# Segment mean over sorted ids: the preparation of the bridges of more groups moved from GpSimd to VectorE

## The chip, the cores and the metric

One core of one Trainium2 chip runs the kernel. The metric is the device time of one execution in microseconds (us); the figure for a kernel is the median of its runs.

## What is computed

```python
data = np.random.randn(10_000_000).astype(np.float32)
segment_ids = np.sort(np.random.randint(0, 10000, 10_000_000))
np.add.at(sums, segment_ids, data)
np.add.at(counts, segment_ids, 1)
return sums / np.maximum(counts, 1)
```

The ids are sorted, so a segment is a run of neighbouring elements. The output is one mean for each of the 10,000 segments.

## The kernel before, in words

Each of the 128 partitions holds 78,125 neighbouring elements. They are cut into 90 rows of 875 elements; two rows are one data tile, and there are 45 tiles, 23 even ones and 22 odd ones. The kernel treats a row as holding at most one border between two segments; whether it does is told from samples of the ids ("probes", every 175th id). It has to know at which column of each row the border lies. Then VectorE makes one masked sum per row (`split`, line 662, 90 instructions of 875 columns), and ScalarE makes the plain sum of each tile (`total`, line 650, 45 instructions).

The column of a border is found with the ids themselves, but only with the short stretch of them in which it must lie. For an even tile's row this is `first_look`: a few small VectorE instructions (lines 431 to 475) work out from the probes the address of a window of 175 ids in every partition and write it to IDX; GpSimd then issues an indirect DMA for that row (`gather`, line 415), and ScalarE sums the ids that land (`add_ids`, line 502). `second_look` (line 513, VectorE) turns the sum into the column KK of the border. For an odd tile's row no window is looked up from probes alone: a **bridge** is laid between the even tiles on both sides. `bridge` (lines 566 to 613, VectorE) draws a line between the columns of the neighbours, which gives the address of a window of 232 ids (IDX, line 605); GpSimd gathers it, ScalarE sums it, and `bridged` (line 624, VectorE) makes the column of it.

The rows are taken in nine groups of up to three even tiles (GROUPS, line 41). Group g has an even part, `look`, `ids` and `second`, and, from group 1 on, an odd part, `prepare`, `bridge`, `xids` and `bridged`, for the odd tiles between its even tiles and those of the group before. The gathers of one full part are six indirect DMAs. In the text, "even 5" is the even part of group 5 and "odd 4" the odd part of group 4.

`prepare(i, j)` (lines 521 to 555) makes four small tiles that `bridge` needs and that hang on the probes alone: LN, SM, FB and WV, 128 partitions by 4 or 6 columns. It has two forms. If `i < EARLY`, VectorE makes them in four instructions (lines 532 to 540). Otherwise GpSimd makes them in six (lines 545 to 553). Here i is the number of the first odd tile of the group. With line 1274, `put(f"prepare{g}", prepare(o0, o1))`, and line 1268, `o0, o1 = max(i - 1, 0), j - 1`, it is 0, 2, 5, 8, 11, 14, 17 and 20 for groups 1 to 8. With EARLY = 5 (line 162), groups 1 and 2 are prepared by VectorE and groups 3 to 8 by GpSimd.

```python
            if i < EARLY:
                v = nc.vector
                v.tensor_scalar(
                ...
                return
            e = nc.gpsimd
```

The order of work on every engine is written out by hand. TIMES (lines 42 to 152) gives each step a number, and the steps are put in the order of these numbers; the whole part of a number is the split after which the step comes, so that "prepare4" at 22.02 stands right behind "second4" at 22.02, and ahead of the third step of "look5" at 22.035. An engine runs its own instructions in that order. On GpSimd, the gathers of a part and the six instructions of a `prepare` stand in one queue: prepare 3 stands between the gathers of even 4 and of odd 3, and prepare 4 between those of odd 3 and of even 5.

The gathers write into a ring of 18 slots (GT). The data tiles come into 16 buffers by SyncE's queue, in the order of ORDER (line 36), with the loads of the probes among them. After the last split the pieces are put together: TensorE folds shifted copies (lines 1058 to 1074), `hits` (lines 634 to 642) and `spread` (line 1129) come on GpSimd behind the last gathers, and `ends` (line 1227) on VectorE writes the last columns of the output.

Of the kernel before, what the change touches and what calls it, by code (L numbers as in the profile page):

```python
# [158 lines left out]
R1 = 8 * M1 - 2  # L159
R2 = NR + 4  # L160
RM = 74
EARLY = 5
LATE = [r for r in range(RM, NR, 4)]
C1, CA, C2 = 31, 67, 48

# [70 lines left out]
def kernel(  # L236
# [68 lines left out]
    def view(ap, dims):  # L305
        return bass.AP(ap.tensor, ap.offset, [list(ap.ap[0])] + dims)
# [214 lines left out]
    def prepare(i, j):  # L521

        def s1():
# [5 lines left out]
            ids = view(pr32[:, 4 * i + 2, 0:1], [[8 * K, n], [2 * K, 2]])  # L529
            if i < EARLY:  # L530
                v = nc.vector
# [822 lines left out]
```

## Time and profile before

| | us |
|---|---|
| median of 3 runs | 186.96 |
| lowest and highest run | 186.78, 187.04 |
| the profiled execution | 187.27 |
| its span, first to last instruction | 185.5 |
| outside the span | 1.8 |

Busy within the span: VectorE 138.3 us, ScalarE 122.9, GpSimd 115.5, TensorE 15.9.

In the profile's rows, PE is TensorE's matmuls, DVE is VectorE, ACT ScalarE, POOL GpSimd, and SP SyncE; L415 is line 415 of the kernel. Times are us from the start of the span. A row of a timeline begins with start and duration; what stands in brackets at its end is the time for which the engine sat idle just before, and what ended that. A wait that the profile can't put down to an instruction is called "issue". A gather's duration on POOL is the time in which its descriptors are written, not that in which its bytes arrive.

### The profile page before, as it was taken

The numbers are of one execution on the slowest core, as the hardware profiler recorded it, in microseconds if no ns is written. First come the engines' busy times: TensorE is split into PE (matmuls) and PEld (weight loads), VectorE is DVE, ScalarE is ACT, GpSimd is POOL, SyncE is SP. The second block draws the span as 40 slices with busy tenths as digits, with TensorE's granted clock in tenths as the row PEclk, the third lists the DMA queues.
The fourth block names the chain that finished last, engine by engine and source line by source line (L and its number), as shares of the span: only waits on it lengthen the run. The fifth ranks groups of instructions, "written<-read, shape, count | busy, mean of one in ns | idle before, by whom it ended". The sixth has DMA issues, their size and how long they took to land.

```text
span 185.5 us, 1564 instructions
## 1 busy us (share of the span) xinstructions
PE 15.9 (9%) x72; PEld 15.6 (8%) x72; DVE 138.3 (75%) x466; ACT 122.9 (66%) x290; POOL 115.5 (62%) x166
## 2 busy tenths in 40 slices
PE   0000000000000000010000000000000065009900
PEld 0000000000000000010000000000000065009900
DVE  6314396980349999192999999696999999699980
ACT  8503655640599995392997985567889686989700
POOL 5474757787577287777468777737838788552400
DMA  5999999999999999999999999999999999940000
GB/s 110 114 272 287 202 264 399 238 410 344 341 394 334 350 396 334 339 331 337 404 328 340 394 329 386 388 398 411 411 403 402 397 408 404 409 207 0 0 4 12
DMA packets 47685, 56.71 MB, mean 306 GB/s; under 512 B 37664, under 2 KB 38104, under 8 KB 47671
## 3 DMA queue, kind: packets, MB, share of 16 engines
q1 hardware_dynamic: 41739, 40.32, 65.8%
q0 software_dynamic: 5760, 16.26, 26.1%
q14 instruction: 13, 0.11, 0.2%
q10 hardware_dynamic: 172, 0.00, 0.1%
q8 instruction: 1, 0.02, 0.0%
HBM read 58.97 MB, written 0.04 MB: 318 GB/s over the span
## 4 chain that ended last, share of the span: by engine, by line
DMA 36%; issue 18%; POOL 15%; ACT 11%; DVE 8%; PE 5%; SPq 4%; POOLq 0%; DVEq 0%; ACTq 0%
DMA GT<-in_segment_ids_dram,IDX 32%; POOL GT L415 11%; ACT junk_a L650 6%; ACT junk_i L502 5%; PE outp L1070 5%; DMA pr<-in_segment_ids_dram 4%; DVE junk_v L662 4%; SPq L272 3%; SPq L290 1%; POOL xa L1129 1%; SPq L277 1%; DVE most L1203 1%; DVE pa L1112 0%; POOL bad L875 0%; DVE j L838 0%
## 5 line engine op out<-in xcount | busy, mean ns | idle before, releaser
L415 POOL DMA_INDIRECT GT<-in_segment_ids_dram,IDX x90 | 92.8, 1031 | 46.0 <-issue 24.2
L662 DVE SCALAR_TENSOR_TENSOR junk_v<-iota,q,data_t 128x875 bf16<-128x875 f32 x90 | 98.8, 1116 | 0.3 <-DVE SG L458 0.2
L650 ACT ACTIVATE junk_a<-data_t 128x1750 bf16<-128x1750 f32 (+1 forms) x45 | 73.7, 1639 | 1.1 <-issue 0.7
L502 ACT ACTIVATE junk_i<-GT 128x175 bf16<-128x175 int32 (+1 forms) x90 | 33.6, 374 | 49.6 <-DMA GT<-in_segment_ids_dram,IDX 46.7
L502 ACT ACTIVATION_READ_ACCUMULATOR junk_i<-GT 128x1 f32 x90 | 16.8, 187 | 0.0
L513 DVE SCALAR_TENSOR_TENSOR q<-YY,GS 128x6 f32<-128x6 f32 (+2 forms) x9 | 1.5, 169 | 16.8 <-ACT junk_i L502 14.6
L1058 PE MATMUL outp<-tab,diag 128*128 128x79 f32 x24 | 5.4, 424 | 66.3 <-DVE tab L1038 66.3
L1058 PEld LDWEIGHTS outp<-tab,diag 128*128 128x128 f32 x24 | 5.2, 331 | 66.4 <-DVE tab L1038 66.4
L1070 PE MATMUL outp<-xa,ident 128*128 128x36 f32 x40 | 8.7, 408 | 11.1 <-POOL xa L1129 11.1
L1070 PEld LDWEIGHTS outp<-xa,ident 128*128 128x128 f32 x40 | 8.6, 332 | 11.3 <-POOL xa L1129 11.3
L431 DVE TENSOR_TENSOR q<-pr 128x12 f32<-128x12 int32 (+3 forms) x9 | 1.6, 176 | 10.1 <-DMA pr<-in_segment_ids_dram 9.8
L650 ACT ACTIVATION_READ_ACCUMULATOR junk_a<-data_t 128x1 f32 x45 | 8.4, 187 | 0.0
L769 PE MATMUL small<-q,ident 128*128 128x100 f32 x2 | 0.7, 464 | 82.8 <-DVE q L761 82.8
L769 PEld LDWEIGHTS small<-q,ident 128*128 128x128 f32 x2 | 0.5, 314 | 82.8 <-POOL WV L553 82.8
L624 DVE TENSOR_TENSOR q<-ZV,GS 128x6 f32<-128x6 f32 (+1 forms) x8 | 1.3, 166 | 8.2 <-ACT junk_i L502 8.2
L662 DVE DVE_READ_ACCUMULATOR junk_v<-iota,q,data_t 128x1 f32 x90 | 7.4, 82 | 0.0
L308 ACT ACTIVATE GT<-q 128x4176 int32<-128x4176 f32 x1 | 3.9, 3894 | 0.0
L681 DVE TENSOR_TENSOR q<-T,q 128x10 f32<-128x10 f32 (+3 forms) x5 | 2.1, 412 | 1.5 <-ACT junk_a L650 1.5
L1157 POOL TENSOR_TENSOR pb<-pb,RB 128x620 f32<-128x620 f32 x1 | 1.3, 1315 | 2.2 <-DVE RB L937 2.2
L638 POOL TENSOR_TENSOR uu<-uu,GS 128x44 f32<-128x44 f32 x1 | 0.3, 279 | 3.3 <-ACT junk_i L502 3.3
L1196 POOL TENSOR_TENSOR add<-gg,XX 128x620 f32<-128x620 f32 x1 | 1.3, 1302 | 1.4 <-DVE XX L1189 1.4
L1047 DVE TENSOR_TENSOR diag<-ident,dm 128x1664 f32<-128x1664 f32 x1 | 1.9, 1891 | 0.0
(159 smaller groups left out, 84.0 us busy)
## 6 DMA issues: line engine op xcount, KB each, us to landing
data_t<-in_data_dram SPq DMA_DIRECT2D x44, 875.0 KB
GT<-in_segment_ids_dram,IDX POOLq DMA_INDIRECT x90
data_t<-in_data_dram SPq DMA_DIRECT2D x1, 562.5 KB
pr<-in_segment_ids_dram SPq DMA_DIRECT2D x22, 11.0 KB
pr<-in_segment_ids_dram SPq DMA_DIRECT2D x3, 6.0 KB
out_dram<-OUT SPq DMA_DIRECT2D x1, 36.6 KB
pr<-in_segment_ids_dram SPq DMA_DIRECT2D x1, 4.0 KB
snt<-in_segment_ids_dram ACTq DMA_DIRECT2D x1, 1.0 KB
```

The lines of the kernel that those rows point to most:

```text
L272: nc.sync.dma_start(out=pr_flat[:, a:b], in_=ids_p[:, a * S : (b - 1) * S + 1 : S])
L277: nc.sync.dma_start(out=pr_flat[:, a:b:w], in_=ids_p[:, a * S : (b - 1) * S + 1 : w * S])
L290: nc.sync.dma_start(out=d[:, 0 : b - a], in_=data_p[:, a:b])
L308: nc.scalar.activation(out=gt32[:, :, 0 : 2 * WO : 2], in_=view(q5[:, 0, 0:1], [[0, RING], [0, WO]]), func=ACT.Copy)
L415: nc.gpsimd.indirect_dma_start(out=GT[:, slots[r], 0:w], out_offset=None, in_=ids2d[:], in_offset=bass.IndirectOffsetOnAxis(ap=IDX[:, r : ...
L502: nc.scalar.activation(out=turned(junk_i)[:, 0:w], in_=gt32[:, slots[r], 0 : 2 * w : 2], func=ACT.Copy, accum_out=GS[:, r : r + 1],)
L650: nc.scalar.activation(out=junk_a[:, 0:n], in_=tiles[t][:, 0:n], func=ACT.Copy, accum_out=T[:, 2 * t : 2 * t + 1])
L662: nc.vector.scalar_tensor_tensor(out=turned(junk_v)[:, 0:n], in0=iota[:, 0:n], scalar=KK[:, r : r + 1], in1=d, op0=ALU.is_ge if r % 2 else ...
L681: nc.vector.tensor_sub(out=odd(A), in0=even(T), in1=even(A))
L1047: nc.vector.tensor_tensor(out=diag, in0=view(ident[:, 0:1], [[0, ND], [1, P]]), in1=view(dm[:, 0:1], [[1, ND], [0, P]]), op=ALU.mult,)
L1058: nc.tensor.matmul(out=outp[:, 0:NO], lhsT=diag[:, d], rhs=tab[:, d : d + NO], start=d == 0, stop=False)
L1070: nc.tensor.matmul(out=outp[:, C1:CA], lhsT=ident[:, 0:P], rhs=xa[:, :, r - R1], start=False, stop=False)
```

## The change

One constant is raised from 5 to 9:

```diff
@@ -159,7 +159,7 @@
 R1 = 8 * M1 - 2
 R2 = NR + 4
 RM = 74
-EARLY = 5
+EARLY = 9
 LATE = [r for r in range(RM, NR, 4)]
 C1, CA, C2 = 31, 67, 48
```

The constant is used in one place, the condition in `prepare` that is quoted above. It was announced as: the bridges of the last four groups, too, are prepared by VectorE in four fused steps instead of six on GpSimd; nothing else is changed.

## Rows read from the trace of the kernel before

**Rows 1.** The waits of the whole span: who, for whom, total, times, longest
```profile
ACT junk_i L502 <- DMA GT<-in_segment_ids_dram,IDX: 46.7, 30, 9.1
DVE q L513 <- ACT junk_i L502: 14.6, 4, 8.2
```

**Rows 2.** The chain that ended last: start, duration, what
```profile
79.64 7.90 DMA GT<-in_segment_ids_dram,IDX
...
119.34 7.28 DMA GT<-in_segment_ids_dram,IDX
...
155.28 7.82 DMA GT<-in_segment_ids_dram,IDX
```

**Rows 3.** Windows: us, PE, PEld, DVE, ACT, POOL busy, PEclk, DMA share, GB/s
```profile
70.00:80.00 10.00, 0.00 (x0) 0.00 (x0) 5.61 (x15) 4.83 (x17) 7.57 (x13) 1.00 1.10 324
160.00:170.00 10.00, 3.29 (x16) 3.29 (x16) 8.04 (x27) 9.38 (x18) 4.18 (x8) 1.00 0.47 191
```

**Rows 4.** The page's part on DMA queues: the gathers' queue, packets, MB, share
```profile
q0 software_dynamic: 5760, 16.26, 26.1%
```

**Rows 5.** Timeline of VectorE: instructions that waited, over the middle of the span
```profile
55.42 0.17 DVE L624 TENSOR_TENSOR q<-ZV,GS 128x4 f32<-128x4 f32 x1 [2.35 <-ACT junk_i L502]
...
78.33 0.20 DVE L624 TENSOR_TENSOR q<-ZV,GS 128x6 f32<-128x6 f32 x1 [4.36 <-ACT junk_i L502]
...
88.10 0.21 DVE L513 SCALAR_TENSOR_TENSOR q<-YY,GS 128x6 f32<-128x6 f32 x1 [3.32 <-ACT junk_i L502]
...
118.61 0.17 DVE L624 TENSOR_TENSOR q<-ZV,GS 128x6 f32<-128x6 f32 x1 [1.44 <-ACT junk_i L502]
...
127.19 0.18 DVE L513 SCALAR_TENSOR_TENSOR q<-YY,GS 128x6 f32<-128x6 f32 x1 [1.37 <-ACT junk_i L502]
...
162.30 0.17 DVE L681 TENSOR_TENSOR q<-T,q 128x10 f32<-128x10 f32 x1 [1.47 <-ACT junk_a L650]
```

**Rows 6.** Line 545, the first of GpSimd's six: durations, first and last start
```profile
L545 POOL TENSOR_SCALAR LN<-NBP x6: 195/204/206, 58.2 to 146.5; 128x6 f32<-128x6 f32 x5, 128x4 f32<-128x4 f32 x1
```

**Rows 7.** Timeline of GpSimd: around prepare 3 and prepare 4
```profile
63.23 1.12 POOL L415 DMA_INDIRECT GT<-in_segment_ids_dram,IDX  x1 [3.44 <-DVE IDX L605]
...
69.88 1.00 POOL L415 DMA_INDIRECT GT<-in_segment_ids_dram,IDX  x1 [0.30 <-issue]
70.95 0.20 POOL L545 TENSOR_SCALAR LN<-NBP 128x6 f32<-128x6 f32 x1
...
73.01 1.10 POOL L415 DMA_INDIRECT GT<-in_segment_ids_dram,IDX  x1 [0.59 <-DVE junk_v L662]
...
79.64 1.00 POOL L415 DMA_INDIRECT GT<-in_segment_ids_dram,IDX  x1 [0.30 <-issue]
```

**Rows 8.** Timeline of VectorE: prepare 2 begins, and the instruction behind it
```profile
25.84 0.16 DVE L532 TENSOR_SCALAR LN<-NBP 128x6 f32<-128x6 f32 x1
...
26.13 0.16 DVE L470 SCALAR_TENSOR_TENSOR ST<-NBP,ST 128x6 f32<-128x6 f32 x1
```

**Rows 9.** Timeline of VectorE: addresses of even 5, bridge 4's last steps
```profile
68.48 0.17 DVE L475 SCALAR_TENSOR_TENSOR IDX<-ST,wb 128x6 int32<-128x6 f32 x1
...
80.63 0.17 DVE L599 TENSOR_SCALAR CC<-CC 128x6 f32<-128x6 f32 x1
...
80.83 0.17 DVE L605 SCALAR_TENSOR_TENSOR IDX<-CC,FB 128x6 int32<-128x6 f32 x1
```

**Rows 10.** Timelines: a long VectorE instruction, and the gather beside it
```profile
38.27 1.89 DVE L1047 TENSOR_TENSOR diag<-ident,dm 128x1664 f32<-128x1664 f32 x1
...
38.50 2.54 POOL L415 DMA_INDIRECT GT<-in_segment_ids_dram,IDX  x1 [0.30 <-issue]
```

**Rows 11.** Timeline of ScalarE: last id sums of even 5 and even 7, one total
```profile
87.62 0.36 ACT L502 ACTIVATE junk_i<-GT 128x175 bf16<-128x175 int32 x1 [2.67 <-DMA GT<-in_segment_ids_dram,IDX]
...
109.78 1.66 ACT L650 ACTIVATE junk_a<-data_t 128x1750 bf16<-128x1750 f32 x1 [0.72 <-issue]
...
126.71 0.36 ACT L502 ACTIVATE junk_i<-GT 128x175 bf16<-128x175 int32 x1 [0.95 <-DMA GT<-in_segment_ids_dram,IDX]
```

## The prediction

> **What bounds the kernel now.** I read four views in this order: the waits, the chain that ended last, the windows, and then the timelines of VectorE, GpSimd and ScalarE around the places where the change works.
>
> The waits show a loop. ScalarE waits 46.7 us in 30 times for gathered ids to land, and VectorE then waits 14.6 us in 4 times for ScalarE's sum of them [rows 1]. The chain that ended last runs through the same loop: it contains the last gather of even 5, issued at 79.64 and landed 7.90 us later, that of even 7 at 119.34 (7.28 us) and that of odd 8 at 155.28 (7.82 us) [rows 2]. VectorE writes addresses, GpSimd issues six gathers, they land, ScalarE sums, VectorE works out the next addresses. The reader is to see that this latency is the bound, and that no engine's share of busy time is.
>
> The second candidate is the transfer as such. From 70 to 80 us the DMA engines are busy all the time (share 1.10) [rows 3]. But they are done early: from 160 to 170 the share is 0.47 [rows 3], so the data stream ends near 165, while the span runs to 185.5. And in the middle VectorE's idle time before its waiting instructions ends with a sum of ScalarE, not with a data tile [rows 5]. I take the loop to be the bound, and the stream to be close behind it.
>
> **What the change does.** The text announces the last four groups. The code says otherwise: the condition compares i, the first odd tile, with EARLY, and i is 0, 2, 5, 8, 11, 14, 17, 20. Raising 5 to 9 moves the groups with i = 5 and i = 8, that is groups 3 and 4, and leaves the last four (11 to 20) on GpSimd. Before, line 545 runs 6 times [rows 6]; after, it must run 4 times. Twelve small GpSimd instructions go and eight VectorE instructions come. No DMA and no other instruction moves.
>
> **Removed from GpSimd, prepare 3.** It stands ahead of the gathers of odd 3. The first of these waits at 63.23, after 3.44 us of idleness, for VectorE's address [rows 7]. Taking away work ahead of a wait of 3.44 us gains nothing: 0.
>
> **Removed from GpSimd, prepare 4.** It stands between the last gather of odd 3 and the first of even 5. The former begins at 69.88 and takes 1.00, so GpSimd is free at 70.88; prepare 4 starts at 70.95, and the next gather only at 73.01 [rows 7]. Without it the next gather starts after the usual pause of 0.30 us [rows 7], at 71.18. Its address is not what it waits for: line 475 is done at 68.65 [rows 9]. So the first gather of even 5 is issued 73.01 - 71.18 = 1.83 us sooner. The last one follows five gathers later, each 1.00 with a pause of 0.30 [rows 7]: 71.18 + 5 x 1.30 = 77.68 instead of 79.64. The first gather after other work takes 1.10 instead of 1.00 [rows 7], and that goes too. I count **1.9 us** for the issue of the last gather.
>
> **Added to VectorE.** Prepare 2 has this form already: four instructions from 25.84, and the next one starts at 26.13 [rows 8], so 0.29 us each time, 0.6 us together. Prepare 3 comes behind split 13, right ahead of the 2.35 us in which VectorE waits for odd 1 until 55.42 [rows 5]: hidden. Prepare 4 comes behind line 513 of group 4 and pushes line 475 from 68.48 to about 68.8 [rows 9], still 2.4 us ahead of GpSimd's 71.18; the splits behind it run into the 4.36 us of waiting until 78.33 [rows 5]: hidden. Without these two covers the cost would be up to 0.6 us.
>
> **Interference.** Small VectorE instructions will now run while GpSimd writes the descriptors of odd 3. A long one hurts: beside line 1047 (1.89 us) a gather took 2.54 instead of 1.00 [rows 10]. Small ones don't: the gather at 79.64 took 1.00 [rows 7] while the steps of bridge 4 that end with those at 80.63 and 80.83 were running [rows 9]. Bounds: 0, and 0.29 us if all four instructions stop the gather. I take 0, since the nearer row is that of the same small tiles. The Trainium skill, "SBUF — State Buffer", section "Who interferes with whom", speaks against the change here: VectorE's tensor_scalar can take the port pair that GpSimd needs, and an instruction with two SBUF inputs contends with a GpSimd instruction that reads SBUF. By that rule the gain would shrink by up to the 0.29 us just bounded.
>
> **What comes of 1.9 us.** The last gather of even 5 begins at 79.64 and ScalarE sums its ids at 87.62, 7.98 us later, after waiting 2.67 us for them [rows 7, 11]. The last one of even 7 needed 126.71 - 119.34 = 7.37 us [rows 2, 11]. So the sum of even 5 moves by 1.9 us if the latency stays, and by 7.98 - 7.37 + 1.9 = 2.5 us if it gets that of even 7. I take the middle, **2.2 us**, as I can't see which transfers it will meet. VectorE waits there 3.32 us until 88.10 [rows 5], so it can use all of that, and at most 3.3.
>
> **Who is late next.** Behind 88.10, VectorE writes the addresses of even 6, and these feed the next gathers; all the later waits, 1.44 us at 118.61, 1.37 at 127.19 and 1.47 at 162.30 [rows 5], end with work that hangs on gathers issued after 88.10. Odd 4 gains less: GpSimd would be ready about 1.9 us sooner, but its address is written at 80.83 [rows 9], behind a wait that nothing moves. It costs nothing, as VectorE does not wait for odd 4. So everything behind 88.10 moves forward together, with one weak place: the total at 109.78 already waited 0.72 us for what I take to be its data tile [rows 11]. That stops ScalarE for a moment; the waits behind it are longer than this.
>
> **Sum.** 0 (prepare 3) - 2.2 (prepare 4) + 0 (VectorE) + 0 (interference). Against the profiled execution: span 185.5 - 2.2 = 183.3, with 1.8 outside it 185.1 instead of 187.27. That execution lies 0.3 above the median of the runs; the median goes from 186.96 to **184.8 us**.
>
> **Rivals.**
> - *The gathers stand in the DMA engines anyway* (chance 0.16). For it: the DMA share of 1.10 and the latency of 7.98 us [rows 3, 7, 11], against a writing time of 1.00. If the queue is what takes the time, gathers issued 1.9 us sooner wait 1.9 us longer, and 88.10 stays. Against it: the latency is nearly the same, 7.3 to 8.0 us, in three places with quite different issue patterns [rows 2], and even 5 stands behind odd 3 by a pause of 2 us. Time: 186.96, within 0.3 us.
> - *The data stream takes over, slower* (chance 0.08). The gathers use 26.1% of the DMA time [rows 4]. If they run 1.9 us ahead, the stream gets up to 0.26 x 1.9 = 0.5 us later. Its place is ScalarE's totals, of which the one at 109.78 waits already; it decides if the totals at the end, too, wait for data. Then the gain is gone and the end moves by 0.5 us: 187.5. Against it: the stream is over near 165, 20 us ahead of the end of the span.
> - *The change doesn't do what it says.* By the code this is certain in part: two groups move, and they are not the last. The forecast is made for these two.
>
> **How the numbers follow.** About 0.2% (0.37 us) is what a measurement of this kernel can tell from no change. The forecast, with anything from a gain of 0.4 up to 3.3 us, has 0.76: 183.7 to 186.5. No change has 0.16, slower 0.08. The low end of the range is 186.96 - 3.3 = 183.6, all of VectorE's wait gone. The high end takes in the case of no change with its 0.15 of scatter: 187.1. Left out are the slower case and a gain that later waits enlarge.
>
> **What would show it.** Line 545 four times, the first at about 79 instead of 80.71; no GpSimd instruction between the gathers of odd 3 and even 5, the first of even 5 at about 71.2; VectorE's second look of group 5 near 85.9 instead of 88.10, and its wait of 3.32 shrunk to about 1.1; the waits at 118.61, 127.19 and 162.30 still there, some 2 us sooner. The rival of the queue is right if the gather is issued at 71.2 and the sum of its ids still starts near 87.6. The rival of the stream is right if ScalarE's totals near the end wait. If prepare 3 or 4 shows up as a delay of 78.33, my covers were wrong.

## The result and the profile after

Measured: **185.12 us**, the median of four runs (183.58 to 187.02), beside 186.87 us (186.31 to 187.04) for the kernel before; ratio 0.9837, 95% interval 0.9809 to 0.9865. A second measurement gave 184.21 us (six runs) beside 186.22 (26 runs), ratio 0.9879 (0.9829 to 0.9928). The forecast was 184.8 us, between 183.6 and 187.1, and faster.

The runs of one kernel spread over up to 4 us, the kernel before included (183.37 to 187.36 in its 26 runs), and the ratios leave out runs more than 1.5% above a kernel's fastest, so the experiments below also give the median of all runs.

The profiled execution of after is one of its long ones: 187.02 us, span 185.2. Its span is only 0.3 us below that of before, so it does not show the gain at the end. It does show the mechanism, and where the gain can go.

Line 545, the first of GpSimd's six steps, now runs four times (before: [rows 6]). Two groups have moved, and they are not the last four.

```profile
L545 POOL TENSOR_SCALAR LN<-NBP x4: 195/204/206, 77.9 to 146.6; 128x6 f32<-128x6 f32 x3, 128x4 f32<-128x4 f32 x1
```

The timeline of GpSimd at the place of [rows 7]: last gather of odd 3, then even 5's first and last, then the preparation that now comes first.

```profile
69.02 1.00 POOL L415 DMA_INDIRECT GT<-in_segment_ids_dram,IDX  x1 [0.30 <-issue]
70.33 1.00 POOL L415 DMA_INDIRECT GT<-in_segment_ids_dram,IDX  x1 [0.30 <-DVE junk_v L662]
...
76.85 1.00 POOL L415 DMA_INDIRECT GT<-in_segment_ids_dram,IDX  x1 [0.31 <-issue]
77.92 0.21 POOL L545 TENSOR_SCALAR LN<-NBP 128x6 f32<-128x6 f32 x1
```

Nothing stands between the gathers any more. Even 5 follows 1.31 us behind the start of odd 3's last gather; before it was 73.01 - 69.88 = 3.13. To even 5's last gather it is 7.83 us instead of 79.64 - 69.88 = 9.76, so 1.93 less.

The timeline of VectorE, second look of group 4 (66.22), the bridged step of odd 3 (75.82), second look of group 5 (83.17), and behind it splits that wait for a data tile. The columns are those of [rows 5].

```profile
66.22 0.16 DVE L513 SCALAR_TENSOR_TENSOR q<-YY,GS 128x6 f32<-128x6 f32 x1
75.82 0.17 DVE L624 TENSOR_TENSOR q<-ZV,GS 128x6 f32<-128x6 f32 x1 [2.34 <-ACT junk_i L502]
...
83.17 0.17 DVE L513 SCALAR_TENSOR_TENSOR q<-YY,GS 128x6 f32<-128x6 f32 x1 [1.07 <-ACT junk_i L502]
...
91.69 1.13 DVE L662 SCALAR_TENSOR_TENSOR junk_v<-iota,q,data_t 128x875 bf16<-128x875 f32 x1 [1.15 <-DMA data_t<-in_data_dram]
...
96.96 1.13 DVE L662 SCALAR_TENSOR_TENSOR junk_v<-iota,q,data_t 128x875 bf16<-128x875 f32 x1 [3.08 <-DMA data_t<-in_data_dram]
...
127.32 0.17 DVE L513 SCALAR_TENSOR_TENSOR q<-YY,GS 128x6 f32<-128x6 f32 x1 [2.06 <-ACT junk_i L502]
```

The look that stood at 88.10 with a wait of 3.32 [rows 5] comes 4.93 us sooner. Only a part of this can come from prepare 4: group 4's look was 0.79 us earlier already (before: 67.01), and odd 3's bridged step, whose gathers stand ahead of prepare 4 in the queue, 2.51 us earlier (before: 78.33 [rows 5]). From that step to the look it takes 7.35 us instead of 9.77, 2.42 less, and the wait ahead of the look is 1.07 instead of 3.32. At 127.32 nothing of the gain is left (before: 127.19). In between, VectorE and ScalarE wait for data tiles, which no row of before names. The costliest groups of the page (busy us, mean ns | idle us before, and what ended most of it):

```profile
L662 DVE SCALAR_TENSOR_TENSOR junk_v<-iota,q,data_t 128x875 bf16<-128x875 f32 x90 | 99.1, 1116 | 6.2 <-DMA data_t<-in_data_dram 5.8
L650 ACT ACTIVATE junk_a<-data_t 128x1750 bf16<-128x1750 f32 (+1 forms) x45 | 73.8, 1641 | 10.3 <-DMA data_t<-in_data_dram 9.6
```

The waits of ScalarE for gathered ids went the other way, from 46.7 us in 30 times [rows 1] to:

```profile
ACT junk_i L502 <- DMA GT<-in_segment_ids_dram,IDX: 34.4, 24, 7.9
```

So ScalarE waits 12.3 us less for ids and 9.6 us for data. Two windows of 5 us show where the stream falls back, with the columns of [rows 3]; first after:

```profile
75.00:80.00 5.00, 0.00 (x0) 0.00 (x0) 3.94 (x19) 4.58 (x10) 3.54 (x9) 1.00 1.05 375
80.00:85.00 5.00, 0.99 (x4) 0.93 (x4) 3.93 (x13) 3.49 (x11) 3.92 (x4) 1.00 0.86 196
```

and the same windows of the kernel before:

```profile
75.00:80.00 5.00, 0.00 (x0) 0.00 (x0) 1.64 (x7) 2.67 (x7) 3.78 (x5) 1.00 1.12 300
80.00:85.00 5.00, 0.99 (x4) 0.93 (x4) 4.44 (x16) 3.54 (x12) 3.77 (x9) 1.00 0.98 381
```

From 80 to 85 us the DMA engines were busy for 0.86 of the time, but moved 196 GB/s instead of 381: (381 - 196) x 5 = 0.93 MB less. Just ahead of that they had moved 375 instead of 300, 0.38 MB more. Over the ten us 0.55 MB came later, more than half a data tile (0.9 MB), while the steps that use the data came sooner. Why the stream fell back stays open.

### The profile page after: what moved, and what is told of

It reads as the page before. It is cut to its first block, busy times and chain, and to the rows that moved or that the text cites. A ratio compares the mean times of both kernels' runs of the same rounds, so it can differ in the third digit from the quotient of the medians.

```text
span 185.2 us, 1553 instructions
## 1 busy us (share of the span) xinstructions
PE 15.9 (9%) x72; PEld 15.6 (8%) x72; DVE 138.6 (75%) x474; ACT 123.6 (67%) x290; POOL 112.8 (61%) x154
## 4 chain that ended last, share of the span: by engine, by line
DMA 37%; issue 17%; ACT 12%; POOL 9%; DVE 9%; SPq 6%; PE 5%; POOLq 0%; DVEq 0%; ACTq 0%
DMA GT<-in_segment_ids_dram,IDX 23%; DMA data_t<-in_data_dram 11%; POOL GT L415 8%; ACT junk_a L650 7%; DVE junk_v L662 6%; ACT junk_i L502 5%; PE outp L1070 5%; DMA pr<-in_segment_ids_dram 4%; SPq L272 3%; SPq L290 3%; POOL xa L1129 1%; SPq L277 1%; DVE most L1203 1%; DVE most L1227 0%; PE outp L1074 0%
```

## The experiments

Two theories had to be told apart. **Place in the queue**: the gain is that even 5's gathers no longer stand behind prepare 4 on GpSimd. **The stream**: whatever the gathers gain, the data tiles cap it. Twelve runs were made; two of them are the kernels after and before once more.

### The change again, its two halves, and a change of order alone

The change again (the kernel after, no edit):

> The changed kernel itself, again, for a second profile and more times. Theory A (the loop of gathers, GpSimd's queue): about 183.7 us, and in the profile even 5's first gather near 70 to 71 us, the second look of group 5 some 2 to 5 us sooner than 88.10, and the waits behind it moved with it. Theory B (the data stream takes over): where VectorE and ScalarE wait for data tiles for several us, as in the first profile of the changed kernel (5.8 and 9.6 us), the end is near 187; an execution near 183.7 must show clearly less of it.

Group 4 alone on VectorE:

```diff
-            if i < EARLY:
+            if i < EARLY or i == 8:
```

> Only group 4 (i = 8) is prepared by VectorE; group 3 stays on GpSimd. Theory A: the whole gain comes from prepare 4, which stands between two batches of gathers, so 183.7 +- 0.4 us, the same as the changed kernel. A rival (both groups count, prepare 3 lets odd 3 be asked for sooner): half of the gain or less, 185 us or more.

Group 3 alone on VectorE:

```diff
-            if i < EARLY:
+            if i < EARLY or i == 5:
```

> Only group 3 (i = 5) is prepared by VectorE; group 4 stays on GpSimd. Theory A: prepare 3 stands ahead of a wait of 3.44 us, so nothing changes: 186.9 +- 0.4 us, the first gather of odd 3 still right behind VectorE's address. The rival that both groups count: 185.5 us or less.

Nothing on VectorE, but prepare 4 issued earlier in GpSimd's own queue:

```diff
-    "prepare4": [22.02],
+    "prepare4": [13.025],
```

> No work is taken from GpSimd: with EARLY = 5, prepare 4 is only moved up in GpSimd's queue, right behind prepare 3, where GpSimd waits anyway (step 13.025 instead of 22.02). Theory A (it is the place in GpSimd's queue, not the engine or the number of instructions): the same gain as the changed kernel, 183.7 +- 0.5 us, even 5's first gather 0.3 us behind odd 3's last one. A rival (fewer instructions on GpSimd, or fused ones on VectorE, bring it): near 186.9 us.

Measured, beside 186.22 us for before (26 runs):

```
                     median   runs  range              ratio (95%)
the change again     184.21    6    183.16 to 185.44   0.9879 (0.9829 to 0.9928)
group 4 alone        184.50   10    184.10 to 187.12   0.9979 (0.9928 to 1.0031)
group 3 alone        185.84   12    183.64 to 186.99   0.9951 (0.9889 to 1.0013)
prepare 4 earlier    184.52   11    183.46 to 186.85   0.9975 (0.9911 to 1.0039)
```

By the medians, group 4 alone and the change of order alone each give 1.7 us and group 3 alone 0.4. By the ratios only the whole change is told from 1, so these times point to group 4 and don't prove it. The 183.7 us expected of three of them was that of the short runs of after: the change again came 0.5 us above it, group 4 alone and the change of order 0.8 us, and group 3 alone, at 185.84, lies between the two values named for it. The traces are clearer. In the profile of the change again, an execution of 185.44 us, ScalarE waits 6.7 us and VectorE 3.5 us for data, less than the 9.6 and 5.8 of the longer execution above, as the theory of the stream has it. In the kernel that only changes the order, both preparations run while GpSimd waits for addresses, and even 5 follows odd 3 as in the kernel after:

```profile
58.23 0.20 POOL L545 TENSOR_SCALAR LN<-NBP 128x6 f32<-128x6 f32 x1
...
59.89 0.20 POOL L545 TENSOR_SCALAR LN<-NBP 128x6 f32<-128x6 f32 x1
...
69.93 1.00 POOL L415 DMA_INDIRECT GT<-in_segment_ids_dram,IDX  x1 [0.30 <-issue]
71.23 1.00 POOL L415 DMA_INDIRECT GT<-in_segment_ids_dram,IDX  x1 [0.30 <-issue]
```

It keeps all twelve steps on GpSimd and VectorE's work as it was, so for this gap the engine doesn't matter, the place does. With group 3 alone moved, prepare 4 is still in the way, GpSimd's timeline shows:

```profile
69.08 0.99 POOL L415 DMA_INDIRECT GT<-in_segment_ids_dram,IDX  x1 [0.30 <-issue]
70.14 0.20 POOL L545 TENSOR_SCALAR LN<-NBP 128x6 f32<-128x6 f32 x1
...
72.32 1.12 POOL L415 DMA_INDIRECT GT<-in_segment_ids_dram,IDX  x1 [0.60 <-DVE junk_v L662]
```

and yet VectorE's timeline of this kernel has the second look of group 5 early, with no wait:

```profile
83.55 0.16 DVE L513 SCALAR_TENSOR_TENSOR q<-YY,GS 128x6 f32<-128x6 f32 x1
```

That was a surprise: gathers issued as late as before had landed in time. A single profile of before could therefore be an unlucky landing, and the next runs asked for that.

### The kernel before again, and the work put back

The kernel before, no edit:

> The kernel before, unchanged, as a run of its own. Question: is the landing that held VectorE at 88.10 us in the profiled execution of before (second look of group 5, group 3 alone moved: 83.55) a property of the kernel or of that one execution? Theory 'place in GpSimd's queue': the second look of group 5 stands at 86 to 88.5 us again, the bridged step of group 5 at 118 to 119, and the time is 186 to 187. Theory 'chance of the landing': the second look of group 5 comes anywhere from 83.5 to 88, data tiles are waited for by name wherever it comes early, and the time falls anywhere in the 183.4 to 187.4 us that the earlier runs of this kernel span. Ratio to itself 1.000 within 0.005 under both.

The kernel after, with six steps of the old sizes in prepare 4's old place on GpSimd, writing to tiles that nobody reads (XLN, XSM):

```diff
                 )
+                if i == 8:
+                    e = nc.gpsimd
+                    e.tensor_scalar(
+                        out=own(XLN, i, j), in0=own(NB, i, j), scalar1=-1024.0 * FAR, scalar2=-3.0 * L,
+                        op0=ALU.mult, op1=ALU.add,
+                    )
+                    e.tensor_scalar(out=o(XLN), in0=o(NB), scalar1=128.0 * FAR, scalar2=None, op0=ALU.mult)
+                    e.tensor_tensor(out=o(XLN), in0=o(XLN), in1=o(wb), op=ALU.add)
+                    e.tensor_tensor(out=XSM[:, i:j], in0=each(BT, 4 * i + 2, n), in1=each(BT, 4 * i + 3, n), op=ALU.add)
+                    e.tensor_scalar(out=o(XLN), in0=ids, scalar1=float(WO), scalar2=None, op0=ALU.mult)
+                    e.tensor_tensor(out=o(XLN), in0=o(XLN), in1=o(wb), op=ALU.subtract)
                 return
```

> The kernel after, with six steps of GpSimd of the sizes of the old preparation of group 4 put back in its old place ahead of the last gather of group 5; their results go to tiles that nobody reads. VectorE keeps its four added steps. Theory 'place in GpSimd's queue': the whole gain goes, the first gather of group 5 again starts 1.5 to 2.0 us behind the last of odd group 3, and the time is that of the kernel before (185.8 to 187). Theory 'the data stream sets the end': the steps of GpSimd are covered, and the time stays that of after, 184 to 185. Theory 'six steps on VectorE and GpSimd together cost': slower than before, over 187.2.

Measured, beside 186.36 us for before (35 runs): the kernel before again 185.97 us (12 runs, 183.20 to 187.19), ratio to itself 0.9998 (0.9944 to 1.0053). With the work put back 185.62 us (12 runs, 182.42 to 186.89), ratio 0.9983 (0.9924 to 1.0042). The times point to the gain being gone, and don't prove it: 0.998 is not told from 1 and stands above the 0.988 of the kernel after, but the two intervals touch, the median is a little under the 185.8 expected, and the shortest run, 182.42, is shorter than every run of the kernel after.

VectorE's timeline of before, a second time:

```profile
88.03 0.17 DVE L513 SCALAR_TENSOR_TENSOR q<-YY,GS 128x6 f32<-128x6 f32 x1 [2.40 <-ACT junk_i L502]
```

and GpSimd's with the work put back (its lines are shifted by two, 417 for 415):

```profile
69.86 1.00 POOL L417 DMA_INDIRECT GT<-in_segment_ids_dram,IDX  x1 [0.30 <-issue]
70.94 0.21 POOL L547 TENSOR_SCALAR XLN<-NBP 128x6 f32<-128x6 f32 x1
...
73.11 1.12 POOL L417 DMA_INDIRECT GT<-in_segment_ids_dram,IDX  x1 [0.60 <-issue]
```

The gap is 3.25 us again instead of 1.31, so six steps in this place delay even 5 by 1.94 us. This second profile of before, too, was a long execution (187.19 us), so it doesn't settle whether before's short ones have the look early. No short execution of before was profiled. (The expectation says that the steps stand ahead of the last gather of group 5; they stand ahead of its first.)

### A thinner data stream

Six data tiles are loaded by half, in after and in before:

```diff
+HALF = range(16, 28, 2)
...
+        if k in HALF:
+            b = a + L
         nc.sync.dma_start(out=d[:, 0 : b - a], in_=data_p[:, a:b])
...
+        if ORDER.index(t) in HALF:
+            nc.scalar.activation(
+                out=view(junk_a[:, 0:1], [[L, 2], [1, L]]), in_=view(tiles[t][:, 0:1], [[0, 2], [1, L]]),
+                func=ACT.Copy, accum_out=T[:, 2 * t : 2 * t + 1],
+            )
+            return
...
+        if ORDER.index(r // 2) in HALF:
+            d = tiles[r // 2][:, 0:n]
```

> The kernel after, with six of the 45 data tiles (every second one from the 17th to the 27th in the order of loading) loaded by half: 2.69 MB less. Their second row reads the first row's half, so parts of the sums are left out; all steps of ScalarE and VectorE keep their sizes. Theory 'the data stream gives part of the gain back': no step waits for a data tile by name between 88 and 118 us any more (5.8 us of VectorE's and 9.6 of ScalarE's before), and the time falls by the 1 to 3 us that were given back, to 181 to 183. Theory 'the gathers alone set the end': the time stays at 184 to 185 apart from what thinner traffic takes off the landing of the gathers, at most 1 us.

> The kernel before with the same six data tiles loaded by half (the same parts of the sums left out). Theory 'the data stream gives part of the gain back': it is not the bound of before, so the time falls by less than that of after does under the same edit, and the two thin kernels lie further apart than the two whole ones (2 us): 2.5 to 4 us. Theory 'the gathers alone set the end': the two thin kernels lie as far apart as the two whole ones, 1.5 to 2.2 us.

Measured: thin after 183.20 us (12 runs, 181.44 to 184.19), ratio 0.9905 (0.9853 to 0.9957); thin before 184.87 us (12 runs, 184.24 to 185.86), ratio 1.0049 (1.0015 to 1.0083). Every run of the first lies below every run of the second, and the medians are 1.67 us apart. The expected 2.5 to 4 us was too much: the pair lies about as far apart as the whole ones do by their medians (186.22 - 184.21 = 2.01), so the times don't show that the stream takes part of the gain. Thin after was expected at 181 to 183 us and came out just above. The traces, one execution each, do show it. The only wait for a data tile that is left in thin after is, in place of 9.6 and 5.8 us:

```profile
ACT junk_a L659 <- DMA data_t<-in_data_dram: 0.6, 1, 0.6
```

VectorE in thin after, the second looks of groups 4, 5 and 7 (in the thin kernels the lines are shifted by three, 516 for 513):

```profile
66.07 0.16 DVE L516 SCALAR_TENSOR_TENSOR q<-YY,GS 128x6 f32<-128x6 f32 x1
...
82.79 0.17 DVE L516 SCALAR_TENSOR_TENSOR q<-YY,GS 128x6 f32<-128x6 f32 x1
...
122.07 0.17 DVE L516 SCALAR_TENSOR_TENSOR q<-YY,GS 128x6 f32<-128x6 f32 x1 [2.72 <-issue]
```

and in thin before:

```profile
67.02 0.16 DVE L516 SCALAR_TENSOR_TENSOR q<-YY,GS 128x6 f32<-128x6 f32 x1
...
85.88 0.17 DVE L516 SCALAR_TENSOR_TENSOR q<-YY,GS 128x6 f32<-128x6 f32 x1 [0.52 <-issue]
...
124.97 0.17 DVE L516 SCALAR_TENSOR_TENSOR q<-YY,GS 128x6 f32<-128x6 f32 x1 [2.11 <-ACT junk_i L505]
```

From group 5's look to group 7's, thin after needs 39.28 us and thin before 39.09. The whole kernel after needed 44.15, the change again 40.89. With a thinner stream nothing is given back in these profiles.

The work put back into the thin kernel (both edits above together):

> The kernel of the six steps put back on GpSimd in the old place of group 4's preparation, with the six data tiles loaded by half (the same parts of the sums left out), so that the data stream disturbs less. Theory 'place in GpSimd's queue': the time of the thin kernel before, 184.4 to 185.1, and the first gather of group 5 starts 1.9 us later behind the last of odd group 3 than in the thin kernel after. Theory 'something else in the change gives the gain' (fewer preparations in all, or chance ahead of 50 us): the time of the thin kernel after, 182.9 to 183.3.

Measured: 184.13 us (6 runs, 183.57 to 185.35), in between the two expectations and nearer to the first. It ran on another chip than thin after and thin before, so the trace weighs more here. Even 5's first gather starts 3.25 us behind odd 3's last one, in thin after 1.30: 1.95 us later, as the theory of the place has it. VectorE, the look of group 4, the bridged step of odd 3 and the look of group 5:

```profile
65.85 0.16 DVE L518 SCALAR_TENSOR_TENSOR q<-YY,GS 128x6 f32<-128x6 f32 x1
74.80 0.17 DVE L640 TENSOR_TENSOR q<-ZV,GS 128x6 f32<-128x6 f32 x1 [1.70 <-ACT junk_i L507]
...
85.21 0.17 DVE L518 SCALAR_TENSOR_TENSOR q<-YY,GS 128x6 f32<-128x6 f32 x1 [4.05 <-ACT junk_i L507]
```

Here VectorE is early at 65.85 and 74.80, and then waits 4.05 us for even 5. Thin after, 0.22 us later at group 4's look, did not wait there at all. This is the clearest single picture of what prepare 4 costs in its old place, though still one execution of each.

### The change as it was announced

All preparations on VectorE (EARLY = 99 in the kernel after), whole and thin; and, in the thin kernel before, the last four groups alone:

```diff
-            if i < EARLY:
+            if i < EARLY or i > 8:
```

> The kernel after, with the preparations of the last four groups on VectorE as well, as the announcement of the change has it: GpSimd prepares nothing. Theory 'place in GpSimd's queue': in the profile of the thin kernel after, the preparations of groups 5, 6 and 7 end 0.6 to 0.9 us ahead of the first gather behind them, which starts 0.1, 0.4 and 1.1 us later than the 0.95 us that GpSimd otherwise takes from the address step of VectorE to the first gather; VectorE waits 1.2 to 2.7 us for group 7 further on, so 0.5 to 1.2 us more are gained than by the kernel after: 183 to 184. Theory 'the data stream gives it back': the time of after, 184.2 to 185.1. Theory 'VectorE pays for its steps': 4 groups by 0.29 us on its path, 185.3 to 186.3.

> All preparations on VectorE, with the six data tiles loaded by half (the same parts of the sums left out). Theory 'place in GpSimd's queue': 0.5 to 1.2 us below the thin kernel after (183.2), so 182.0 to 182.7. Theory 'only group 4 stood in the way': 183.2. Theory 'VectorE pays for its steps': 183.8 to 184.4.

> The kernel before with the preparations of its last four groups alone moved to VectorE (groups 3 and 4 stay on GpSimd), which is what the announcement of the change says, with the six data tiles loaded by half (the same parts of the sums left out). Theory 'place in GpSimd's queue': 0.5 to 1.2 us below the thin kernel before (184.9), so 183.7 to 184.4, from the first gathers of groups 6 and 7. Theory 'only group 4 stood in the way': 184.9. Theory 'VectorE pays for its steps': 185.4 to 186.1.

Measured: all on VectorE 184.24 us (6 runs, 183.35 to 184.71) beside 186.42 for before (11 runs), ratio 0.9890 (0.9851 to 0.9928); thin, all on VectorE, 181.14 us (6 runs, 179.97 to 183.05); thin, last four alone, 183.95 us (6 runs, 181.98 to 185.01), 0.9 below thin before, which ran on another chip. Thin, all on VectorE, came out below every value expected for it, 2.1 us under thin after, again from another chip. Thin, all on VectorE, and thin, last four alone, ran on one chip and differ in groups 3 and 4 alone, which is the change of this document: 183.95 - 181.14 = 2.81 us by the medians.

So the groups that were announced seem to give something, about 1 us, but not where I expected it. Groups 6 and 7 show no gain: the look of group 7 stands at 124.94, in thin before at 124.97, and the 38.52 us from group 5's look to it, beside 39.09, lie within what the other thin kernels show. The place where the traces differ is group 8. GpSimd in thin before, last gather of odd 7, prepare 8, first gather of odd 8:

```profile
143.18 1.00 POOL L418 DMA_INDIRECT GT<-in_segment_ids_dram,IDX  x1 [0.31 <-issue]
144.25 0.20 POOL L548 TENSOR_SCALAR LN<-NBP 128x4 f32<-128x4 f32 x1
...
148.99 1.16 POOL L418 DMA_INDIRECT GT<-in_segment_ids_dram,IDX  x1 [0.17 <-issue]
```

and with the last four on VectorE:

```profile
143.38 1.00 POOL L418 DMA_INDIRECT GT<-in_segment_ids_dram,IDX  x1 [0.31 <-issue]
144.43 0.41 POOL L872 TENSOR_SCALAR bad<-base,pin,first 128x1 f32<-128x1 f32 x1
...
147.70 1.14 POOL L418 DMA_INDIRECT GT<-in_segment_ids_dram,IDX  x1 [0.17 <-ACT junk_i L505]
```

From gather to gather it is 4.32 us instead of 5.81: 1.49 us less. Of this the stretch from group 7's look to the last split keeps 1.05 us, as the table below shows; from the last split to the end the kernel then takes 6.8 us instead of 6.4, so about 0.65 us reach the end. All on VectorE, whole, keeps this too, and gives it back in the middle:

```profile
L662 DVE SCALAR_TENSOR_TENSOR junk_v<-iota,q,data_t 128x875 bf16<-128x875 f32 x90 | 99.1, 1117 | 5.5 <-DMA data_t<-in_data_dram 4.5
L650 ACT ACTIVATE junk_a<-data_t 128x1750 bf16<-128x1750 f32 (+1 forms) x45 | 73.9, 1641 | 10.0 <-DMA data_t<-in_data_dram 9.4
```

It is shorter than before and is not told apart from the kernel after (184.21 and 185.12); the theory of the stream had given it 184.2 to 185.1, that of the place 183 to 184.

### All profiles side by side

The span is cut at three of VectorE's steps: the second looks of groups 4, 5 and 7, and the start of the last split. "Late" kernels have six steps of GpSimd between odd 3 and even 5, "early" ones have none: from the start of odd 3's last gather to that of even 5's first it is 3.12 to 3.25 us in all seven late profiles and 1.30 to 1.31 in all seven early ones.

```
                              look 4   4 to 5   5 to 7   7 to last split
late   before                  67.01    21.09    39.09    51.89
late   before again            67.58    20.45    38.90    51.98
late   work put back           67.07    20.14    39.08    51.88
late   group 3 alone           66.28    17.27    40.47    51.79
late   thin before             67.02    18.86    39.09    51.70
late   thin, work put back     65.85    19.36    38.76    51.74
late   thin, last four         67.53    18.89    38.52    50.65
early  after                   66.22    16.95    44.15    51.50
early  the change again        67.53    17.05    40.89    51.78
early  group 4 alone           67.08    17.60    39.29    51.94
early  prepare 4 earlier       67.07    17.76    38.97    51.59
early  all on VectorE          65.50    17.05    41.71    50.71
early  thin after              66.07    16.72    39.28    51.83
early  thin, all on VectorE    67.24    17.90    38.76    50.59
```

Three things are to be read from it. From look 4 to look 5 the late kernels need 19.44 us on the mean, from 17.27 to 21.09, and the early ones 17.29, from 16.72 to 17.90: a difference of 2.15 us, and a third of the spread. Not all of it belongs to prepare 4. Cut once more at odd 3's bridged step, the late kernels need 11.07 us up to it and 8.36 behind it, the early ones 10.67 and 6.62: the difference behind it is 1.74 us. The late kernels there range from 6.42 to 10.41 us, the early ones from 6.20 to 7.47. From look 5 to look 7 all thin kernels need 38.5 to 39.3, and so do the three whole kernels whose look 5 came behind 87 us; of the six whole kernels whose look 5 came early, four need more than 40, up to 44.15. From look 7 on, the three kernels with prepare 8 off GpSimd need 50.6 to 50.7, the others 51.5 to 52.0. Each line is one execution.

## Why the prediction was right

**What it does.** Right: two groups moved, groups 3 and 4, not the last four.

**Prepare 3: 0.** Right within what the runs tell. Group 3 alone gave a median 0.4 us lower, with a ratio interval that holds 1.

**Prepare 4: 1.9 us at the issue.** Right. From the start of odd 3's last gather to even 5's first it is 1.31 us instead of 3.13, and the slower first gather (1.10) went too; to the last gather of even 5 it is 1.93 us less, and putting the work back cost 1.94.

**2.2 us at VectorE's look of group 5.** The size came out, in part by luck. In the two first profiles the wait ahead of the look shrank from 3.32 us to 1.07, just as forecast, and the mean over the fourteen profiles is 1.74 us behind odd 3's bridged step, or 2.15 with what lies ahead of it. But the sum that I made it from does not hold. I took the landing as a latency of 7.4 to 8.0 us. In the profile of after the last gather of even 5 began at 76.85 and its ids were summed at 82.68, only 5.83 us later. With group 3 alone it was 3.93 us (78.96 to 82.89), and a late issue cost nothing at all. The landing varies by more than what is gained. And the wait for odd 3, of which I wrote that nothing moves it, ended at 75.82 instead of 78.33.

**The first rival**, that the gathers stand in the DMA engines anyway, fell: with the gathers issued sooner, the time to the sum of their ids did not grow (5.83 us instead of 7.98), and look 5 came sooner on the mean by about what the issue had gained.

**VectorE's eight steps: 0, hidden.** Right as far as seen. Line 475 came 1.78 us behind group 4's look (66.22, 68.00) instead of 1.47 (67.01, 68.48 [rows 9]), the 0.3 us expected, and still ahead of the gather at 70.33. With 16 more of them (all on VectorE, thin) the look of group 7 came at 123.90, behind a wait of 2.06 us.

**Interference: 0.** Right. In after, prepare 4's steps on VectorE run right beside a gather; VectorE's first of four, then GpSimd:

```profile
66.30 0.17 DVE L532 TENSOR_SCALAR LN<-NBP 128x6 f32<-128x6 f32 x1
```

```profile
66.41 1.00 POOL L415 DMA_INDIRECT GT<-in_segment_ids_dram,IDX  x1 [0.30 <-issue]
```

The gather took its usual 1.00 us. The rule of the Trainium skill ("SBUF — State Buffer", "Who interferes with whom") that VectorE's tensor_scalar can take the port pair which GpSimd needs cost nothing here. But these rows test it weakly, as that tensor_scalar ended 0.06 us after the gather had begun; what VectorE can do to a gather stands in the last section.

**Everything behind 88.10 moves along.** This step failed, and the forecast held in spite of it: in the profile of after nothing of the gain was left at group 7's look. I saw one weak place, the total at 109.78 with its 0.72 us [rows 11], and took it to be covered. In fact ScalarE had 9.6 us and VectorE 5.8 us of waits for data in the profile of after, from 88 to 118 us. My second rival named this mechanism; I gave it a chance as a loss only, and looked for it at the end of the span, where the DMA share is low [rows 3]. It works in the middle, as a cap on the gain: in the five early whole kernels the stretch from look 5 to look 7 lost between 0 and 5 us against the 39 us of the thin ones. What the cap costs the median is not shown: the thin pair lies no further apart than the whole one. Over many runs something near the forecast is left: the medians of after lie 1.75 and 2.01 us below those of before.

**The base.** I compared with 186.96 us and a scatter of 0.15 us, from three runs. In 26 and 35 runs before itself spreads from 183.3 to 187.4. The forecast of the difference held, but the first comparison, in which every run of before was a long one, was a lucky draw; the bounds of 0.2% that I gave for what can be told were too narrow for this kernel, where even 12 runs leave an interval of half a per cent to either side.

What stays open: whether the short executions of before are those in which even 5 happens to land early. Group 3 alone and the late kernels' spread in the table speak for it. It was not shown. Open, too, is how much of the gain in the time of the whole kernels is group 4's alone; that rests on the traces, on the thin pair, and on the two thin kernels that differ in groups 3 and 4.

## What to carry to other kernels

Work on an engine that also issues DMAs costs what stands behind it in that engine's queue, not what the engine's busy share says: six steps of 0.2 us in front of gathers whose addresses were ready cost 1.9 us, six like them in front of gathers still waiting for an address cost nothing that the runs could tell, and moving them within the same queue closed the same gap as moving them to another engine. When one latency goes, look at the next resource at that place and not at the end of the span, and price it as a cap on the gain, too. A single profile of a kernel bound by DMA landings is one draw: profile it several times, and cut the span at fixed steps, before a difference of 2 us is given a cause.

## What the runs showed of the hardware

In these traces a longer TENSOR_TENSOR of VectorE (0.91 and 1.89 us) holds a gather that begins behind its start until it ends. In before, line 1047 ended at 38.27 + 1.89 = 40.16 and the gather beside it, from 38.50, at 41.04 [rows 10], 0.88 us later. In after a gather got in 0.27 us ahead of line 1047 and kept its 1.00 us; the next one was held, as VectorE's line 1047 and then GpSimd's two gathers show:

```profile
38.93 1.89 DVE L1047 TENSOR_TENSOR diag<-ident,dm 128x1664 f32<-128x1664 f32 x1
```

```profile
38.66 1.00 POOL L415 DMA_INDIRECT GT<-in_segment_ids_dram,IDX  x1 [0.30 <-issue]
39.96 1.73 POOL L415 DMA_INDIRECT GT<-in_segment_ids_dram,IDX  x1 [0.30 <-issue]
```

It ended at 41.69, 0.87 us behind line 1047 (40.82). Another TENSOR_TENSOR of the same profile, and GpSimd's gather beside it, ended as far apart, at 134.17 and 135.04:

```profile
133.26 0.91 DVE L1112 TENSOR_TENSOR pa<-KL,jj 128x720 f32<-128x720 f32 x1
```

```profile
133.40 1.64 POOL L415 DMA_INDIRECT GT<-in_segment_ids_dram,IDX  x1 [0.30 <-DVE KL L1099]
```

Two fp32 inputs in SBUF are not enough to hold a gather. The splits, SCALAR_TENSOR_TENSOR instructions of 1.12 us, have two as well (iota and data_t), and in before 36 gathers began inside a split with more than 0.3 us of it to go; none took over 1.16 us. The one at 69.88, which took 1.00 us [rows 7], began beside this row of VectorE in before:

```profile
69.69 1.12 DVE L662 SCALAR_TENSOR_TENSOR junk_v<-iota,q,data_t 128x875 bf16<-128x875 f32 x1
```

Which of two gathers line 1047 catches decides between a loss of 1.54 us and one of 0.73, ahead of all that the change touches. The section of the Trainium skill named above infers that tensor_tensor does not stop the writing of descriptors; these rows differ, and the rows decide.
